# A two-layer encoder trunk on one core: the first norms' sums ahead, x fetched one product later, next weights split in front of the turning

## The chip, the cores and the metric

The kernel runs on one core of one Trainium2 chip. The metric is the device time of one execution in microseconds (us). Five engines work beside each other: PE (TensorE; PEld is its weight load), DVE (VectorE), ACT (ScalarE), POOL (GpSimd), and SP, which here only issues DMAs.

## The reference

A trunk of two layers over x of 512 tokens by 1024 features. Layer 0 is a latent attention (MLA), layer 1 a chunked attention over a shared key/value band; each is followed by a SwiGLU FFN with 2816 hidden features. Every sublayer is x + post_norm(f(pre_norm(x))).

```python
def rms_norm(x, g):
    xf = x.astype(jnp.float32)
    y = xf * lax.rsqrt(jnp.mean(xf * xf, axis=-1, keepdims=True) + EPS)
    return (y * g.astype(jnp.float32)).astype(x.dtype)
...
def swiglu(h, w_gate, w_up, w_down):
    return (jax.nn.silu(h @ w_gate) * (h @ w_up)) @ w_down
...
def mla_mixer(h, cos, sin, w_a, g_q, w_uq, g_kv, w_ukv, w_o):
    a = h @ w_a
    cq, ckv, kr = jnp.split(a, [Q_LORA, Q_LORA + KV_LORA], axis=-1)
    q = (rms_norm(cq, g_q) @ w_uq).reshape(B, S, MLA_HEADS, NOPE_DIM + ROPE_DIM)
...
def shared_kv(x, g_src, w_kv):
    kv = (rms_norm(x, g_src) @ w_kv).reshape(B, S, 2, B_HEADS, B_HEAD_DIM)
```

## The kernel before

**Splits.** Every fp32 operand is split into two fp32r halves: ACT casts the high half (L144, tiles named whi, xh, ph), DVE subtracts it from the source and so makes the low half (L145, names wlo, xl, pl). Where a gain is multiplied in, the lines are L148 on ACT and L149 on DVE. A product is three matmuls on PE (L356 to L358, in the FFN's down stage L1185). So a weight tile must pass a DMA into "raw" or "wd", ACT and DVE before PE can use it.

**Order.** All is written as one program; a framework gives each engine a fixed order of instructions by a running priority number, and puts in the waits. `with first(n)` lowers the number for what is written inside it, so that it goes n places earlier on its engine. Each engine then works its row in order: an instruction that waits holds all that is behind it on that engine.

**The start of layer 0** (L773 to L802). While x and w_a arrive, three banks of a first projection are summed over eight tiles of x. `sx.add(x[k])` squares the tile on ACT (L425, sq) and adds it to acc on DVE (L426). `sx.total()` turns acc on PE with four transposes (L435, tot <- ident, acc), and DVE reduces that (L437) to one sum for each token. `rstd` then makes v (L448) on DVE and v^-0.5 on POOL (L452). The second norm, that of the key/value latent, has its own acc and tot and needs the first result (`rstd_of_scaled`, L458 to L462). The result r is spread over partitions by eight PE transposes (L469, bc <- ident, r), behind the rest of the first projection. In between DVE makes the rotary angles (L804 to L823, rot).

**The down stage of the first FFN** (L1163 to L1187). It is seven products (a Strassen-type scheme) in the order A11, A22, A12, E1, E2, E3, E6, each of 66 matmuls of 128x512 that go in groups (0), (1), (2), (3), (4, 5). Results stand in bank pairs al, ga, be, de. E2, E3 both go to al, E6 goes to be. When a product has ended, `one` copies its two banks into new y tiles (L1246, ACT) or adds them to one (L1252, DVE); E3's first matmul into al needs E2's copy out of al. `during(j, i)` runs behind each group: in E2 it fetches x (eight DMAs of 256 KB on SP's queue, L614), in E6 it puts out the four scalings of the first tokens' y (L1304, ACT; they stand as a list in `later`), and at group 3 `turn(0)`: y's first 256 tokens are turned by 16 PE transposes (L1325, yt), DVE adds gain times yt to x (L1328), and the new x is split (xh, xl). For the other 256 tokens the same follows behind E6, with L1295, L1298 and L1289 for its norm.

**What comes next.** Layer 1 begins with the projection of V from x (w_v, four raw tiles, and the first of in_w_qkb), fed by `feed`, which loads and splits weight tiles in the order of their use; `feed.ahead(n)` splits n tiles ahead. A tile of in_w_qkb is also multiplied by a gain on DVE in place (L306) before its split. Raw tiles share five buffers.

Of the kernel before, what the change touches and what calls it, by code (L numbers as in the profile page):

```python
# [18 lines left out]
D, S, P = 1024, 512, 128  # L19
# [3 lines left out]
QL, KVL = 384, 256  # L23
# [45 lines left out]
def trunk(ctx: ExitStack, tc: tile.TileContext, a, out):  # L69
# [25 lines left out]
    def small(name="sm"):  # L95
        return sp.tile([P, 4], F32, tag="small", name=name_(name))
# [38 lines left out]
    @contextmanager  # L135
    def first(n):

        tc.cur_priority -= n
        yield
        tc.cur_priority += n  # L140
# [46 lines left out]
    class Down:  # L187
# [26 lines left out]
        def fetch(self, to, i, q, tag):  # L214
            n, src = self.width(i), self.src[q, i]
            if tag in ("u", "h"):
                parts = []
                for c in range(0, n, S):
                    t = U(name="wd") if tag == "u" else wide[0].tile([P, S], F32, tag="h", name=name_("wd"), bufs=2 * NF - 4)
                    nc.sync.dma_start(t, src[:, c:c + S])  # L220
                    parts.append(t)
            else:
                t = (wp if tag == "raw" else wide[0]).tile([P, 1024], F32, tag=tag, name=name_("raw"),
                                                           bufs=5 if tag == "raw" else 2)
                nc.sync.dma_start(t[:, :n], src[:, :n])
                parts = [t[:, :n]]
            self.at[to, i] = parts
# [121 lines left out]
    feed = Feed()  # L349
# [29 lines left out]
    def some(gen, n):  # L379
        for _ in range(n):  # L380
            next(gen, None)
# [58 lines left out]
    def rstd(ss, n, eps=EPS):  # L440
        parts = ss if isinstance(ss, list) else [ss]
        m = sum(p.shape[1] for p in parts)
        v = small("v")[:, :m]
        w = m // len(parts)
        for i, p in enumerate(parts):
            o = v[:, i * w:(i + 1) * w]
            if eps is EPS:
                V.tensor_scalar(o, p, 1.0 / n, EPS, op0=OP.mult, op1=OP.add)  # L448
            else:
                V.scalar_tensor_tensor(o, p, 1.0 / n, eps[:, i * w:(i + 1) * w], op0=OP.mult, op1=OP.add)  # L450
        r = small("r")[:, :m]
        nc.gpsimd.tensor_tensor(r, v, mhalf[:, :m], op=OP.pow)  # L452
        return r

    def rstd_of_scaled(ss, n, r0):

        v = small("v2")
        V.tensor_tensor(v, ss, r0, op=OP.mult)  # L458
        V.tensor_tensor(v, v, r0, op=OP.mult)
        r = rstd(v, n)  # L460
        o = small("r2")
        V.tensor_tensor(o, r, r0, op=OP.mult)  # L462
        return o

    def spread(col, first=0):

        b = bank("t", "bc")
        for i in range(col.shape[1]):
            nc.tensor.transpose(b[:, (first + i) * P:(first + i + 1) * P],  # L469
                                col[:, i:i + 1].to_broadcast([P, P]), ident)  # L470
        return b
# [300 lines left out]
    xs, sx = [], Sum()  # L772
# [16 lines left out]
    skv = Sum()  # L789
# [5 lines left out]
        nc.scalar.activation(t, b1[j], AF.Copy, scale=g_kv[:, j:j + 1])  # L795
        ckv.append(t)
    some(rest, 2)
    r0 = rstd(sx.total(), D)
    some(rest, 2)
    rkv = rstd_of_scaled(skv.total(), KVL, r0)  # L800

    quarters = [U(name="rot") for _ in range(2)]  # L802
    pos, ang, da, db, t1, t2 = (quarters[n // 4][:, n % 4 * P:(n % 4 + 1) * P] for n in range(6))
# [37 lines left out]
    rkv = spread(rkv)  # L841
# [380 lines left out]
    class After:  # L1222
# [81 lines left out]
                nc.scalar.activation(t, t, AF.Copy, scale=r)  # L1304

        def during(self, j, i):
            if j == Down.E2 and i == 2:
                self.x = fetch(a["mid"])
                self.split = Split(self.x, None)
            if j == Down.E6 and i == 3:  # L1310
                self.turn(0)
            elif j == Down.E6 and self.later:
                with first(60):
                    self.later.pop(0)()

        def turn(self, h):

# [151 lines left out]
    x, sx = post.x, post.split  # L1469
# [230 lines left out]
```

## Time and profile before

| | |
|---|---|
| median of 3 runs | 1128.0 us (1127.02 to 1128.33) |
| profiled execution, its own time | 1128.58 us |
| its span, first to last instruction | 1126.8 us |
| mean granted TensorE clock | 0.998 |
| PE busy | 1109.3 us, 98% |
| PEld busy | 984.4 us, 87% |
| DVE busy | 932.5 us, 83% |
| ACT busy | 685.3 us, 61% |
| POOL busy | 69.6 us, 6% |

The span lies 1.8 us under the execution's own time; that rest is outside the first and the last instruction. A matmul of 128x512 is shown as 0.39 us long but they follow each other every 0.23 us, so distances between starts tell more than busy time.

### The profile page before, as it was taken

The page shows a single profiled execution, that of the slowest core. Times are in us where ns is not written, and L with a number is a line of the kernel's source. Part 1 is how long each engine was busy: PE and PEld are TensorE (multiplying, and loading weights), DVE is VectorE, ACT ScalarE, POOL GpSimd, SP SyncE. Part 2 cuts the span into 40 slices and gives each one's busy share as a digit, 9 for nine tenths or more (in the row PEclk, how much of TensorE's full clock was granted, in tenths as well). Part 3 has the DMA queues.
Part 4 walks back from the last instruction along what each step waited for, and adds up shares of the span by engine and source line. Part 5 has one row for each costly group of instructions (what it writes and reads, how often), then busy time and mean ns, then how long its engine had stood idle before and what let it go on. Part 6 is the DMA issues. An engine that isn't in the chain of part 4 may idle for free.

```text
span 1126.8 us, 18993 instructions
## 1 busy us (share of the span) xinstructions
PE 1109.3 (98%) x6973; PEld 984.4 (87%) x6973; DVE 932.5 (83%) x1671; ACT 685.3 (61%) x1339; POOL 69.6 (6%) x106
## 2 busy tenths in 40 slices
PE   9999999999999999999999999999999999999997
PEld 6788889999999998887888887779999999998885
DVE  7788737999899889978857977647999899889977
ACT  6476637755555566668536777546755555566675
POOL 2200000000000002400000000000000000002402
PEclk9999999999999999999999999999999999999999
DMA  7332125323332449861456656625323322459923
GB/s 235 110 110 81 70 76 205 132 89 99 105 103 95 140 150 256 138 205 41 165 150 172 154 153 159 170 86 184 134 92 95 113 94 95 141 168 286 171 58 76
DMA packets 62990, 150.85 MB, mean 134 GB/s; under 512 B 8432, under 2 KB 10224, under 8 KB 62896
## 3 DMA queue, kind: packets, MB, share of 16 engines
q1 hardware_dynamic: 55552, 136.61, 38.6%
q0 software_dynamic: 6912, 12.59, 6.8%
q8 instruction: 55, 0.90, 0.3%
q10 hardware_dynamic: 432, 0.44, 0.1%
q14 instruction: 39, 0.32, 0.1%
HBM read 119.52 MB, written 9.63 MB: 115 GB/s over the span
## 4 chain that ended last, share of the span: by engine, by line
PE 44%; DVE 5%; ACT 2%; issue 2%; DMA 1%; POOL 0%; POOLq 0%; DVEq 0%; ACTq 0%
PE al L1434 6%; PE b L356 6%; PE b L357 6%; PE b L358 6%; PE al L1185 4%; PE be L1434 4%; PE be L1185 3%; PE ga L1434 2%; PE pt L508 2%; PE de L1185 1%; PE ga L1185 1%; DVE wlo L145 1%; DVE raw L174 1%; DMA raw<-in_w_pair 1%; PE b L1558 1%
## 5 line engine op out<-in xcount | busy, mean ns | idle before, releaser
L144 ACT CAST whi<-raw 128x1024 fp32r<-128x1024 f32 (+3 forms) x224 | 225.5, 1008 | 227.3 <-PE al L1434 74.5
L145 DVE TENSOR_TENSOR wlo<-raw,whi 128x1024 fp32r<-128x1024 f32 (+3 forms) x224 | 260.7, 1165 | 63.0 <-ACT whi L144 61.2
L1434 PE MATMUL al<-th,whi 128*128 128x256 f32 x432 | 123.4, 286 | 0.2 <-DVE ut L1446 0.2
L1434 PE MATMUL al<-th,wlo 128*128 128x256 f32 x432 | 121.4, 281 | 0.0
L1434 PE MATMUL al<-tl,whi 128*128 128x256 f32 x432 | 121.1, 280 | 0.0
L356 PE MATMUL b<-xh,whi 128*128 128x512 f32 (+1 forms) x304 | 116.8, 384 | 0.2 <-ACT xh L148 0.2
L357 PE MATMUL b<-xl,whi 128*128 128x512 f32 (+1 forms) x304 | 113.3, 373 | 0.4 <-DVE xl L149 0.3
L358 PE MATMUL b<-xh,wlo 128*128 128x512 f32 (+1 forms) x304 | 112.8, 371 | 0.0
L174 DVE TENSOR_TENSOR raw<-raw,raw 128x1024 f32<-128x1024 f32 x72 | 86.5, 1218 | 1.3 <-DMA raw<-in_w_pair 1.1
L1434 PEld LDWEIGHTS al<-th,whi 128*128 128x128 f32 x432 | 81.4, 188 | 3.1 <-DVE ut L1446 1.2
L1434 PEld LDWEIGHTS al<-th,wlo 128*128 128x128 f32 x432 | 81.4, 188 | 0.3 <-DVE wlo L145 0.3
L1434 PEld LDWEIGHTS al<-tl,whi 128*128 128x128 f32 x432 | 81.4, 188 | 0.0
L496 ACT ACTIVATE p<-p,mn 128x128 f32<-128x128 f32 (+1 forms) x96 | 54.0, 562 | 31.8 <-DVE mn L494 31.6
L145 DVE TENSOR_TENSOR ptl<-pt,pth 128x128 fp32r<-128x128 f32 (+1 forms) x96 | 46.2, 485 | 28.8 <-ACT pth L144 23.2
L144 ACT CAST whi<-wd 128x512 fp32r<-128x512 f32 x86 | 49.9, 619 | 26.8 <-PE al L1185 11.9
L145 DVE TENSOR_TENSOR wlo<-wd,whi 128x512 fp32r<-128x512 f32 x86 | 56.3, 685 | 11.5 <-ACT whi L144 11.2
L358 PEld LDWEIGHTS b<-xh,wlo 128*128 128x128 f32 x304 | 57.4, 189 | 8.8
L357 PEld LDWEIGHTS b<-xl,whi 128*128 128x128 f32 x304 | 57.5, 189 | 8.5 <-DVE xl L149 1.9
L356 PEld LDWEIGHTS b<-xh,whi 128*128 128x128 f32 x304 | 57.6, 189 | 8.3 <-ACT xh L148 1.3
L144 ACT CAST pth<-pt 128x128 fp32r<-128x128 f32 (+1 forms) x96 | 40.3, 424 | 28.5 <-PE pt L508 27.8
L1185 PE MATMUL al<-whi,ph 128*128 128x512 f32 x132 | 51.9, 393 | 0.5 <-ACT y L1246 0.5
L1185 PE MATMUL al<-whi,pl 128*128 128x512 f32 x132 | 51.5, 390 | 0.0
(309 smaller groups left out, 3264.3 us busy)
## 6 DMA issues: line engine op xcount, KB each, us to landing
raw<-in_w_pair SPq DMA_DIRECT2D x72, 512.0 KB, 3.8
wd<-in_w_down SPq DMA_DIRECT2D x54, 256.0 KB, 5.8
raw<-in_w_o SPq DMA_DIRECT2D x16, 512.0 KB, 3.6
raw<-in_w_gu SPq DMA_DIRECT2D x16, 512.0 KB, 3.6
raw<-in_w_down SPq DMA_DIRECT2D x16, 512.0 KB, 4.3
raw<-in_w_qkb SPq DMA_DIRECT2D x16, 512.0 KB, 3.6
wd<-in_w_down POOLq DMA_DIRECT2D x22, 256.0 KB, 5.8
wd<-raw POOLq DMA_DIRECT2D x22, 256.0 KB, 4.3
```

What stands on the lines that cost most here:

```text
L144: return (nc.scalar.copy(dst_hi, src), V.tensor_tensor(dst_lo, src, dst_hi.bitcast(F32), op=OP.subtract))
L145: V.tensor_tensor(dst_lo, src, dst_hi.bitcast(F32), op=OP.subtract))
L174: V.tensor_tensor(t, x, y, op=OP.add)
L356: nc.tensor.matmul(o, l[0], r[0], start=start, stop=False)
L357: nc.tensor.matmul(o, l[0], r[1], start=False, stop=False)
L358: nc.tensor.matmul(o, l[1], r[0], start=False, stop=stop)
L496: nc.scalar.activation(p[:, :n], p[:, :n], AF.Exp, bias=mn[:, :1], scale=-1.0, accum_out=self.sums[:, qt:qt + 1])
L508: nc.tensor.transpose(t[:, kt * P:(kt + 1) * P], p[:, kt * P:(kt + 1) * P], ident)
L1185: nc.tensor.matmul(to[e], l[c], r[d], start=j < 4 and k == 0 and n == 0, stop=k == NF // 2 - 1 and n == 2, skip_group_check=True)
L1434: nc.tensor.matmul(o, l[c], r[d], start=first_ and n == 0, stop=k == K2 - 1 and n == 2, skip_group_check=True)
L1558: nc.tensor.matmul(o[:, q_], vv, pth[:, kt, q_], start=kt == 0, stop=False)
```

## The change

Four edits. In the start of layer 0, both norms' chains (from the turning of acc to the power) are written in `first(100)`. In the first down stage the eight loads of x are put out in E3 behind group 1, not in E2 behind group 2. At E6's group 3 the next layer's first weights are split (`feed.ahead(2)`) ahead of `turn(0)`. And the scalings of y lose their `first(60)`. The last layer's stage (AfterLast) has its own `during` and is untouched.

```diff
     some(rest, 2)
-    r0 = rstd(sx.total(), D)
+    with first(100):
+        r0 = rstd(sx.total(), D)
     some(rest, 2)
-    rkv = rstd_of_scaled(skv.total(), KVL, r0)
+    with first(100):
+        rkv = rstd_of_scaled(skv.total(), KVL, r0)
...
         def during(self, j, i):
-            if j == Down.E2 and i == 2:
+            if j == Down.E3 and i == 1:
                 self.x = fetch(a["mid"])
                 self.split = Split(self.x, None)
             if j == Down.E6 and i == 3:
+                feed.ahead(2)
                 self.turn(0)
             elif j == Down.E6 and self.later:
-                with first(60):
-                    self.later.pop(0)()
+                self.later.pop(0)()
```

PE, the start of layer 0: where the first norm's four transposes stood and stand (b is the first projection's bank, tot the turned sum of squares; rows with + are the changed kernel's).

```order
 L358 MATMUL b_12_122<-xh_56_279,wlo_54_273 128x512
 L356 MATMUL b_13_123<-xh_56_279,whi_53_272 128x512
+L435 MATMUL tot_78_347<-ident_87,acc_23_152 128x128 x4
 L357 MATMUL b_13_123<-xl_57_280,whi_53_272 128x512
 L358 MATMUL b_13_123<-xh_56_279,wlo_54_273 128x512
```

The four transposes went 20 rows up, into the middle of a sum over x; the second norm's (acc_71) went up by eight. The place of bc on PE is the same in both.

ACT, the end of E2 and the start of E3, before (whi <- wd are high halves of w_down, ph <- hs those of the hidden tiles, y <- al E2's two copies out of the banks that E3 fills next):

```order
L144 CAST whi_1109_5795<-raw_926_4942 128x512
L144 CAST whi_1113_5815<-wd_973_5188 128x512
L144 CAST whi_1113_5815<-wd_974_5190 128x512
L144 CAST ph_1107_5791<-hs_626_2736 128x512
L144 CAST ph_1111_5811<-hs_674_3097 128x512
L144 CAST whi_1121_5851<-wd_981_5216 128x512
L1246 COPY y_1115_5830<-al_946_5100 128x512
L1246 COPY y_1116_5841<-al_947_5101 128x512
```

The same place in the changed kernel, where every line number behind L800 is greater by two:

```order
L144 CAST whi_1101_5779<-raw_926_4942 128x512
L144 CAST ph_1103_5795<-hs_674_3097 128x512
L144 CAST whi_1105_5799<-wd_973_5188 128x512
L144 CAST whi_1105_5799<-wd_974_5190 128x512
L1248 COPY y_1107_5814<-al_946_5100 128x512
L144 CAST whi_1113_5835<-wd_981_5216 128x512
L144 CAST whi_1113_5835<-wd_982_5218 128x512
L1248 COPY y_1108_5825<-al_947_5101 128x512
```

The first copy now stands ahead of the cast of wd_981, the second behind wd_982. On DVE the in-place product of in_w_qkb (L306, raw_1199) went up by 12 rows to the place right ahead of wlo <- wd_973, the first low half that E3 uses, and on SP the load of that tile went ahead of the eight loads of x.

DVE, the last splits of E6 and the first tokens' turning, before (x <- yt are the additions to x, y <- be E3's late addition, wlo_1188 and wlo_1198 the first and second tile of w_v, wv_1200 the third):

```order
L145 TENSOR_TENSOR wlo_1165_6078<-wd_1016_5334,whi_1164_6077 128x512
L1328 SCALAR_TENSOR_TENSOR x_1099_5775<-yt_1166_6093,gains_70,x_1099_5775 128x256
...
L1328 SCALAR_TENSOR_TENSOR x_1106_5789<-yt_1181_6138,gains_70,x_1106_5789 128x256
L1252 TENSOR_TENSOR y_1116_5841<-y_1116_5841,be_951_5105 128x512
L145 TENSOR_TENSOR xl_1178_6130<-x_1103_5783,xh_1177_6129 128x256
L149 SCALAR_TENSOR_TENSOR wlo_1188_6156<-raw_1160_6053,gains_70,whi_1187_6155 128x512 x2
L145 TENSOR_TENSOR xl_1180_6135<-x_1104_5785,xh_1179_6134 128x256
L149 SCALAR_TENSOR_TENSOR wlo_1198_6208<-raw_1163_6075,gains_70,whi_1197_6207 128x512
```

The same place in the changed kernel, where w_v's first tile is called wlo_1168:

```order
L145 TENSOR_TENSOR wlo_1165_6078<-wd_1016_5334,whi_1164_6077 128x512
L149 SCALAR_TENSOR_TENSOR wv_1200_6227<-raw_1166_6093,gains_70,wv_1200_6227 128x512
L149 SCALAR_TENSOR_TENSOR wlo_1168_6096<-raw_1160_6053,gains_70,whi_1167_6095 128x512 x2
L1330 SCALAR_TENSOR_TENSOR x_1121_5881<-yt_1169_6101,gains_70,x_1121_5881 128x256
...
L1330 SCALAR_TENSOR_TENSOR x_1128_5895<-yt_1184_6146,gains_70,x_1128_5895 128x256
L145 TENSOR_TENSOR xl_1183_6143<-x_1126_5891,xh_1182_6142 128x256
L149 SCALAR_TENSOR_TENSOR wlo_1198_6208<-raw_1163_6075,gains_70,whi_1197_6207 128x512
L145 TENSOR_TENSOR xl_1186_6153<-x_1127_5893,xh_1185_6152 128x256
L149 SCALAR_TENSOR_TENSOR wlo_1198_6208<-raw_1163_6075,gains_70,whi_1197_6207 128x512
```

Three scaled subtractions went ahead of all eight additions to x; the second tile's stand behind them still, as before. On ACT the four pairs of whi casts of E6's last groups and the scalings of y (L1304) are mixed now, where two scalings stood ahead of three ph casts and two ahead of all five whi casts; and on PE 12 more of E6's matmuls stand ahead of the first yt.

## Rows read from the trace of the kernel before

**Rows 1.** The page's busy time by engine, and the granted clock in 40 slices.
```profile
PE 1109.3 (98%) x6973; PEld 984.4 (87%) x6973; DVE 932.5 (83%) x1671; ACT 685.3 (61%) x1339; POOL 69.6 (6%) x106
PEclk9999999999999999999999999999999999999999
```

**Rows 2.** Waits of PEld, whole span: what for, us in total, times, longest.
```profile
PEld b L357 <- DVE wlo L149: 1.7, 1, 1.7
PEld yt L1325 <- ACT y L1289: 1.1, 2, 0.8
PEld bc L469 <- issue: 1.1, 1, 1.1
PEld al L1185 <- ACT y L1246: 0.9, 1, 0.9
PEld be L1185 <- ACT whi L144: 0.7, 1, 0.7
```

**Rows 3.** Timeline of PEld, layer 0's start: start, duration, instruction, [wait <- releaser].
```profile
20.31 0.19 PEld L357 LDWEIGHTS b<-xl,whi 128*128 128x128 f32 x1
...
24.85 0.59 PEld L435 LDWEIGHTS tot<-ident,acc 128*128 128x128 f32 x4
...
26.69 0.59 PEld L435 LDWEIGHTS tot<-ident,acc 128*128 128x128 f32 x4
```

**Rows 4.** Timeline of DVE, the same stretch.
```profile
21.21 0.69 DVE L426 TENSOR_TENSOR acc<-acc,sq 128x512 f32<-128x512 f32 x1
...
27.05 0.68 DVE L437 TENSOR_REDUCE ss<-tot 128x4 f32<-128x512 f32 x1
```

**Rows 5.** Timeline of PE at bc.
```profile
31.25 0.39 PE L358 MATMUL b<-xh,wlo 128*128 128x512 f32 x1
32.30 1.06 PE L469 MATMUL bc<-ident,r 128*128 128x128 f32 x8 [0.66 <-DVE r L462]
```

**Rows 6.** Timeline of POOL, the first power.
```profile
28.09 2.07 POOL L452 TENSOR_TENSOR r<-v,mhalf 128x4 f32<-128x4 f32 x1 [12.53 <-DVE v L448]
```

**Rows 7.** Timeline of PEld, the end of E2; ten rows, then two, left out.
```profile
490.96 0.19 PEld L1185 LDWEIGHTS al<-whi,ph 128*128 128x128 f32 x1
...
493.45 0.19 PEld L1185 LDWEIGHTS al<-whi,pl 128*128 128x128 f32 x1
...
494.92 0.19 PEld L1185 LDWEIGHTS al<-whi,pl 128*128 128x128 f32 x1
```

**Rows 8.** Timeline of ACT, the same stretch.
```profile
490.02 1.14 ACT L144 CAST whi<-wd 128x512 fp32r<-128x512 f32 x2 [2.10 <-PE al L1185]
...
493.42 0.62 ACT L144 CAST whi<-wd 128x512 fp32r<-128x512 f32 x1 [1.22 <-PE al L1185]
493.95 1.07 ACT L1246 COPY y<-al 128x512 f32<-128x512 f32 x2
```

**Rows 9.** Timeline of DVE, E2 and E3.
```profile
485.67 1.22 DVE L145 TENSOR_TENSOR wlo<-raw,whi 128x1024 fp32r<-128x1024 f32 x1
...
500.72 1.22 DVE L306 TENSOR_TENSOR raw<-raw,gains 128x1024 f32<-128x1024 f32 x1
```

**Rows 10.** DMAs issued in 484 to 492 us: count, KB each, median us to landing.
```profile
raw<-in_w_v SPq DMA_DIRECT2D x1, 512.0 KB, 5.2
raw<-in_w_qkb SPq DMA_DIRECT2D x1, 512.0 KB, 6.1
```

**Rows 11.** Timeline of DVE, E6 and after.
```profile
521.98 1.26 DVE L1328 SCALAR_TENSOR_TENSOR x<-yt,gains,x 128x256 f32<-128x256 f32 x3
...
528.45 1.41 DVE L149 SCALAR_TENSOR_TENSOR wlo<-raw,gains,whi 128x512 fp32r<-128x512 f32 x2
...
533.47 0.15 DVE L1295 SCALAR_TENSOR_TENSOR ssv<-ss,ssv 128x2 f32<-128x2 f32 x1
```

**Rows 12.** Timeline of PEld, the first matmuls with w_v.
```profile
527.09 0.41 PEld L356 LDWEIGHTS b<-whi,xh 128*128 128x128 f32 x2
529.25 0.19 PEld L357 LDWEIGHTS b<-wlo,xh 128*128 128x128 f32 x1 [1.75 <-DVE wlo L149]
```

## Prediction

> **What bounds the kernel now.** I read the page's busy times first, then the list of PE's waits, then the timelines around the places that the edits touch. PE is busy 98% of the span, and the granted clock is 9 in every slice [rows 1]. So a microsecond is won only where PE stands still, or lost where it is made to. A matmul shown as 0.39 us long hides short stops; the starts show them better: eleven steps from 490.96 to 493.45 us give 0.2264 us for one [rows 7]. In the list of waits five entries lie where the edits are: 1.7, 1.1, 1.1, 0.9 and 0.7 us, 5.5 us in all [rows 2]. That is nearly all that this change can win, and since PE makes up about 0.1 us of each wait of a weight load (it overlaps the matmul ahead), some 5 us at most.
>
> **Step A, the first norms go first.** Before, PE waits at bc for r: from the last matmul's start at 31.25 to bc's at 32.30 are 1.05 us where 0.23 is the step, so 0.82 us are lost [rows 5]. r is late because the first power starts only at 28.09 and takes 2.07 us [rows 6], behind a tot that PE turns at 24.85 and DVE reduces at 27.05 for 0.68 us [rows 3, 4]. With the sums ahead the power starts some 4 us earlier. The second tot goes up by eight rows: 26.69 - 8 x 0.23 = 24.9 us, plus what PE loses ahead of it (next lines), about 26.5 us. From there 0.6 (tot), 0.7 (reduce), about 0.4 for the small products and at most 2.07 for the second power give r at about 30.3 us, while PE comes to bc at 32.9 us. The wait of 0.82 us goes.
>
> But the first tot now stands 20 rows higher, where PE arrives at 20.31 us [rows 3], and its input, acc with the last square of x, is written by DVE from 21.21 for 0.69 us, until 21.90 [rows 4]. Neither ACT's nor DVE's row ahead of that addition changes. Everything behind tot on PE waits with it: 21.90 - 20.31 = 1.6 us, of which 0.1 is made up; I take 1.5 us. Net of A: 1.5 - 0.82 = **+0.7 us**. Bounds: if later stops swallow the delay, because PE is late where it had to wait for something else anyway, -0.8; if the second tot waits as well, for squares that are themselves late by the 1.6 us, +1.2.
>
> The row shows that PE held its clock through the longest of these stops: the wait of 1.7 us before wlo lies in slices that all show 9 [rows 1, 2]. [...]
>
> **Step B, x fetched later.** Three things move with it. On ACT, E2's first copy out of its banks no longer stands behind a cast of wd that is held until 493.42 by PE's own reading of the old tile [rows 8]. Before, the two copies ran from 493.95 to 495.02 and PE's first matmul of E3 came 494.92 - 493.45 = 1.47 us for three steps of 0.23: 0.79 us lost [rows 7]. In the changed kernel the copy can start when E2's first bank is finished, nine matmuls before the product's end, at about 492.1 (491.4 for that weight load, a step and 0.39 us), while ACT is done with the two casts of 490.02 at 491.2 [rows 8]. The second copy, behind the casts of wd_981 and wd_982 (493.42 to 494.5), ends at about 495.1, when PE, seven steps behind 493.45, wants its bank at 495.0. So the 0.79 us go.
>
> Against it: L306, the in-place product of in_w_qkb, now stands on DVE ahead of E3's first low half. Its tile needs the buffer that DVE's split of 485.67 frees at 486.9 [rows 9]. Landings in that stretch took 5.2 to 6.1 us [rows 10], with the eight loads of x among them, which now come later. A tile landing after L us, 1.2 us of product and 0.6 us of split (half of a split of 128x1024 [rows 9]) give the low half at 488.7 + L, and PE wants it at 493.9: no wait up to 5.2 us, 0.9 us at 6.1. Without x's 2 MB in the queue I take 5.2 or less. Net of B: **-0.8 us**, bounds -0.8 and +0.1.
>
> The loads of x themselves have room: their first use is at 521.98 [rows 11], some 20 us behind the new place.
>
> **Steps C and D, the turning.** Scalings later and next weights earlier work at one place. Before, PE loses 0.7 us for a cast of wd that stands behind the scalings on ACT, 1.7 us for w_v's first low half, and 1.1 us for the second tokens' y [rows 2]; less 0.1 to 0.2 us for each, about 3.1 us. After:
> - The 0.7 us: casts and scalings are mixed, the casts of group 3 first, and 12 more matmuls stand ahead of the first turn. I count the 0.6 us won.
> - The 1.7 us: DVE split w_v's first tile at 528.45, behind eight additions and six low halves of x that began at 521.98 [rows 11], so PE's third matmul with w_v came at 529.25 instead of 527.54 [rows 12]. Now that split comes ahead of them. But the second tile's split stays behind them, and three subtractions of 0.7 us each (half of 528.45's pair) are pushed in front of the additions. These start near 521.98 + 2.1 - 0.6 = 523.5 (0.6 because the casts ahead come earlier), and after 6.5 us of the same work and 0.7 us for the split itself the second tile's low half is there at 530.7. PE, 0.6 us earlier, begins the first tile at 526.5, has four turns (about 0.5 us) and 13 steps (2.9 us) to do, and wants it at 529.9. So of 1.5 us lost some 0.7 remain, and a late addition to x may cost PE 0.2 at its third group of turns.
> - The 1.1 us: y waits for a power, and that for L1295 at 533.47 on DVE [rows 11]. The same splits stand ahead of it, so it can come about 1 us earlier, and PE comes earlier by as much: 1.0 us remain.
>
> Lost after: 0.7 + 0.2 + 1.0 = 1.9 us against 3.1: **-1.2 us**. Bounds: -3.1 when all cover is enough, and +0.2 when the additions, now started later, hold PE's turns as long as w_v did.
>
> **Sum.** +0.7 - 0.8 - 1.2 = -1.3 us. The profiled execution's 1128.58 becomes 1127.3; it stands 0.6 us above the median of 1128.0, so the median becomes **1126.7 us**. Against the noise this is small: 0.2% is 2.26 us, about what a measurement of this kernel can tell from no change.
>
> **Rivals.**
> 1. All covers hold and the new wait at tot is swallowed: -0.8 - 0.8 - 3.1 = -4.7 at the most; half of C's and A's doubt resolved this way gives -3, 1125.0 us. For it: in the attention behind layer 0's start PE has its own waits. Against: DVE is at 83% [rows 1] and busiest in exactly this stretch. Chance 0.2.
> 2. The gains are eaten: A's new wait is 1.5 us, and PE just meets the next late row in the down stage. Then about 0, 1128.0 us, between 1127.3 and 1128.9. For it: three stages in series wait for DVE, and moving one row ahead makes the next late. Chance 0.22.
> 3. Slower: in_w_qkb lands late, and DVE, held by L306, holds all of E3's low halves. The wait is L - 5.2 us; to bring -1.3 + (L - 5.2) above +2.26 us, L must pass 8.8 us, where the longest median of that stretch was 6.1 [rows 10]. At 9.5 us: 1128.0 - 1.3 + 4.3 = 1131.0 us. Chance 0.04.
> 4. [...] Chance 0.02. [...]
>
> **How the numbers follow.** The likeliest, 0.52, is -1.3 us, with its own range from 1126.0 to 1127.4. Faster by over 0.2% are rival 1 and a small tail of the likeliest: 0.22. Slower by over 0.2%: rivals 3 and 4, 0.06. Within: 0.72. The range from 1124.6 to 1128.8 us holds the likeliest, rival 2 and the nearer part of rival 1, and leaves out some 0.15.
>
> **What would show it.** A: no wait at bc, a wait of about 1.6 us at the first tot for L426, and r well ahead of PE. B: al's first matmul in E3 at the normal step, L306 done before 493.3. C: no wait of be for whi, a wait of 0.5 to 1 us for the low half of w_v's second tile, about 1 us for the second y. I am wrong if tot's wait is not there (an earlier square), if L306 holds DVE, or if the turning's waits vanish or come back whole.

## The result: 0.24% slower, and where the time went

The changed kernel takes 1130.35 us (median of 20 runs, 1127.34 to 1133.55) against 1127.49 us of before (20 runs, 1126.06 to 1129.05): the ratio is 1.0024, 95% interval 1.0017 to 1.0031. The forecast was 1126.7 us in a range that ended at 1128.8. The profiled execution took 1133.18 us (span 1131.4), so it shows the loss near its largest: 4.6 us of span.

The page of the changed kernel: busy times, and the granted clock.

```profile
PE 1109.9 (98%) x6973; PEld 985.5 (87%) x6973; DVE 932.8 (82%) x1671; ACT 686.2 (61%) x1339; POOL 71.8 (6%) x106
PEclk9999999999999999999899999999999999999999
```

PE is busy only 0.6 us longer than before [rows 1], so the loss is to be looked for in its waits and its clock. One slice of the clock, from 537 to 566 us, shows 8. The list of PEld's waits (what for, us in total, times, longest) says where:

```profile
PEld yt L1327 <- ACT y L1291: 3.5, 1, 3.5
...
PEld tot L435 <- issue: 2.5, 3, 1.9
...
PEld b L357 <- DVE wlo L149: 1.0, 1, 1.0
...
PEld al L1187 <- DVE wlo L145: 0.8, 1, 0.8
```

Against [rows 2]: w_v's wait fell from 1.7 to 1.0, the waits at bc, at E3's first matmul for y, and at E6 for a cast are gone. New are the waits at tot in layer 0's start, 0.8 us at E3's second matmul, and above all 3.5 us for the second tokens' y, where 1.1 us stood in two waits. A wait at a tot of the second layer, at about 775 us, is 1.7 us here and 0.8 us in before; it goes from 0.8 to 2.1 us in the profiles below, 1.4 in that of the fastest version, so it is not counted for or against the edits.

**Start.** PEld in layer 0's start, then DVE's addition that ends acc:

```profile
20.02 0.19 PEld L356 LDWEIGHTS b<-xh,whi 128*128 128x128 f32 x1
22.10 0.42 PEld L435 LDWEIGHTS tot<-ident,acc 128*128 128x128 f32 x4 [1.89 <-issue]
...
26.91 0.42 PEld L435 LDWEIGHTS tot<-ident,acc 128*128 128x128 f32 x4 [0.48 <-issue]
...
33.12 1.01 PEld L469 LDWEIGHTS bc<-ident,r 128*128 128x128 f32 x8
```

```profile
21.30 0.68 DVE L426 TENSOR_TENSOR acc<-acc,sq 128x512 f32<-128x512 f32 x1
```

acc is ready at 21.98, PE came at 20.25 and waited; the second tot waited too. The wait at bc is gone. In before bc's weight load stood here:

```profile
32.27 0.85 PEld L469 LDWEIGHTS bc<-ident,r 128*128 128x128 f32 x8 [1.05 <-issue]
```

It stands at 33.12 now, 0.85 us later, against the 0.7 forecast.

**E2 to E3.** PEld, then DVE, then the load of in_w_qkb (us to landing):

```profile
494.10 0.19 PEld L1187 LDWEIGHTS al<-whi,ph 128*128 128x128 f32 x1
495.09 0.19 PEld L1187 LDWEIGHTS al<-wlo,ph 128*128 128x128 f32 x1 [0.80 <-DVE wlo L145]
```

```profile
493.21 1.23 DVE L306 TENSOR_TENSOR raw<-raw,gains 128x1024 f32<-128x1024 f32 x1 [3.54 <-DMA raw<-in_w_qkb]
```

```profile
raw<-in_w_qkb SPq DMA_DIRECT2D x1, 512.0 KB, 5.7
```

The copy of y no longer holds PE [rows 7, 8], but L306 waited for in_w_qkb, which was issued at 487.35 and landed 5.7 us later. So the gain was given back in this execution.

**E6 and behind.** This is where the time is. DVE, POOL, ACT and PEld around the second tokens' norm:

```profile
533.25 0.16 DVE L1297 SCALAR_TENSOR_TENSOR ssv<-ss,ssv 128x2 f32<-128x2 f32 x1
533.32 0.75 DVE L149 SCALAR_TENSOR_TENSOR wv<-raw,gains,wv 128x512 fp32r<-128x512 f32 x1
533.98 1.22 DVE L145 TENSOR_TENSOR wlo<-raw,whi 128x1024 fp32r<-128x1024 f32 x1
535.12 0.42 DVE L426 TENSOR_TENSOR acc<-acc,sq 128x256 f32<-128x256 f32 x1
535.45 1.22 DVE L306 TENSOR_TENSOR raw<-raw,gains 128x1024 f32<-128x1024 f32 x1
540.26 1.27 DVE L1330 SCALAR_TENSOR_TENSOR x<-yt,gains,x 128x256 f32<-128x256 f32 x3 [3.58 <-PE yt L1327]
```

```profile
533.55 3.68 POOL L1300 TENSOR_TENSOR r<-ssv,mhalf 128x2 f32<-128x2 f32 x1 [19.50 <-DVE ssv L1297]
```

```profile
537.26 2.56 ACT L1291 ACTIVATE y<-y,r 128x512 f32<-128x512 f32 x4 [4.98 <-POOL r L1300]
```

```profile
534.30 0.19 PEld L356 LDWEIGHTS b<-wv,xh 128*128 128x128 f32 x1
538.03 0.29 PEld L1327 LDWEIGHTS yt<-ident,y 128*128 128x128 f32 x2 [3.54 <-ACT y L1291]
```

In the trace of before DVE and POOL did this at the same place:

```profile
533.54 1.41 DVE L149 SCALAR_TENSOR_TENSOR wv<-raw,gains,wv 128x512 fp32r<-128x512 f32 x2
534.86 1.22 DVE L145 TENSOR_TENSOR wlo<-raw,whi 128x1024 fp32r<-128x1024 f32 x1
536.85 1.27 DVE L1328 SCALAR_TENSOR_TENSOR x<-yt,gains,x 128x256 f32<-128x256 f32 x3 [0.77 <-PE yt L1325]
```

```profile
533.77 1.07 POOL L1298 TENSOR_TENSOR r<-ssv,mhalf 128x2 f32<-128x2 f32 x1 [20.12 <-DVE ssv L1295]
```

L1297 is on time, a little before [rows 11]. But POOL's power of 128x2 elements, 1.07 us in before, takes 3.68 us and ends 0.56 us behind the end of L306. y is scaled from then on, and PE stands. And then the clock falls. Windows of 5 us (busy time and count of PE, PEld, DVE, ACT, POOL, then granted clock, DMA share, GB/s):

```profile
534.00:539.00 5.00, 1.89 (x8) 1.27 (x8) 2.67 (x4) 1.74 (x3) 3.23 (x1) 0.81 0.88 306
539.00:544.00 5.00, 5.00 (x16) 3.99 (x15) 2.72 (x7) 4.59 (x14) 0.00 (x0) 0.51 0.53 198
```

Windows of 1 us show 1.00 at 536 us, 0.54 at 537, 0.50 in each of the five from 538 to 543, 0.55 at 543, and 1.00 again at 544. Means of 0.81 and of 0.51 over 5 us each are then (0.19 + 0.49) x 5 / 0.5 = 6.8 us at 0.50, which costs at most 3.4 us of work; PE still stood idle in the first microsecond of it. At 0.50 PE's matmuls of 128x512 start 0.43 us apart (541.08, 541.51, 541.94 us), where 0.23 is the step.

So the theory, called P: the power waits for the row of two-input operations on DVE, which the two edits of E6 have changed: one operation of L149's kind in place of two, and L426 and L306 in front of the pause. Its rivals: the earlier splits make the norm late (Q); tot's wait is the loss and the rest is noise (R); the power is long because of the loads that land then (S).

### The profile page after: what moved, and what is told of

Read it like the earlier page. It is cut to its first block, busy times and chain, and to the rows that moved or that the text cites. A ratio compares the mean times of both kernels' runs of the same rounds, so it can differ in the third digit from the quotient of the medians.

```text
span 1131.4 us, 18991 instructions
## 1 busy us (share of the span) xinstructions
PE 1109.9 (98%) x6973; PEld 985.5 (87%) x6973; DVE 932.8 (82%) x1671; ACT 686.2 (61%) x1339; POOL 71.8 (6%) x106
## 4 chain that ended last, share of the span: by engine, by line
PE 82%; DVE 7%; ACT 4%; DMA 3%; issue 2%; POOL 1%; POOLq 0%; DVEq 0%; SPq 0%; ACTq 0%
PE al L1436 15%; PE b L356 10%; PE b L357 10%; PE b L358 10%; PE be L1436 8%; PE al L1187 6%; PE ga L1436 4%; PE be L1187 4%; PE de L1187 3%; PE ga L1187 3%; PE pt L508 2%; DVE wlo L145 2%; ACT whi L144 1%; DMA raw<-in_w_akv 1%; DVE raw L174 1%
## 5 line engine op out<-in xcount | busy, mean ns | idle before, releaser
L145 DVE TENSOR_TENSOR wlo<-raw,whi 128x1024 fp32r<-128x1024 f32 (+3 forms) x224 | 261.2, 1167 | 62.5 <-ACT whi L144 60.6
L145 DVE TENSOR_TENSOR ptl<-pt,pth 128x128 fp32r<-128x128 f32 (+1 forms) x96 | 46.2, 486 | 28.7 <-ACT pth L144 23.0
L145 DVE TENSOR_TENSOR wlo<-wd,whi 128x512 fp32r<-128x512 f32 x86 | 56.5, 688 | 10.8 <-ACT whi L144 10.6
L1187 PE MATMUL al<-wlo,ph 128*128 128x512 f32 x132 | 51.5, 390 | 0.4 <-DVE wlo L145 0.4
```

Of the source, the lines that this page charges most:

```text
L145: V.tensor_tensor(dst_lo, src, dst_hi.bitcast(F32), op=OP.subtract))
L1187: nc.tensor.matmul(to[e], l[c], r[d], start=j < 4 and k == 0 and n == 0, stop=k == NF // 2 - 1 and n == 2, skip_group_check=True)
```

## Experiments

All stand against before on the same chip; microseconds won or lost against before are worked out from the ratio. The edits are called a (norms first), b (x fetched later), c (weights split ahead), d (scalings without head start).

**c alone.**

```diff
             if j == Down.E6 and i == 3:
+                feed.ahead(2)
                 self.turn(0)
```

> The kernel before with one edit alone: the next layer's first weights split ahead of the first tokens' turning. Theory P (POOL's second power of this stage, 3.68 us in the changed kernel against 1.07, waits while DVE runs two-input operations back to back): here DVE's row behind the second norm's sum is as before, a scaled subtraction and one split and then a pause, so the power takes 1.0 to 1.7 us and PE's wait for the scaled y stays under 1.5 us; PE's wait for w_v's low half falls from 1.7 to about 1 us; time 0 to 1 us below before. Rival Q (the earlier weight splits themselves push the norm of the second tokens back): the power's input comes 1 to 2 us later, the wait for y grows to 2 to 3 us, time 1 to 2 us above before.

1126.58 us, ratio 0.9993 (0.9984 to 1.0001). The power takes 1.07 us, and PE's wait for w_v's low half falls to 1.0 us. DVE, then POOL:

```profile
533.03 1.41 DVE L149 SCALAR_TENSOR_TENSOR wv<-raw,gains,wv 128x512 fp32r<-128x512 f32 x2
534.35 1.21 DVE L145 TENSOR_TENSOR wlo<-raw,whi 128x1024 fp32r<-128x1024 f32 x1
```

```profile
533.25 1.07 POOL L1298 TENSOR_TENSOR r<-ssv,mhalf 128x2 f32<-128x2 f32 x1 [20.36 <-DVE ssv L1295]
```

Two operations of L149's kind stand behind the sum here, as in before; in the changed kernel only one does. Q falls: the splits stand earlier, and the norm is not late.

**d alone.**

```diff
-                with first(60):
-                    self.later.pop(0)()
+                self.later.pop(0)()
```

> The kernel before with one edit alone: the scalings of y without their head start. DVE's row behind the second norm's sum gets one addition of squares in front of the additions to x, but not the product of in_w_qkb. Theory P: the power may wait for the split and that addition, 1 to 2.3 us; E6's wait for a cast of w_down (0.7 us) goes; time -0.7 to +0.8 us against before. Rival Q (late scalings make the first turning late): a wait of 1 us or more of PE at the first turns, time 1 us above before.

1127.23 us, ratio 0.9999 (0.9990 to 1.0008). E6's wait of 0.7 us for a cast is gone, but w_v's wait grows from 1.7 to 2.1 us, as PE comes earlier to the same late split. The power takes 1.07 us, again beside two operations of L149's kind.

**c and d together.** Both edits above.

> The two edits of E6 together (weights split ahead of the turning, scalings without head start), without the norms' edit and without the later fetch of x. Only with both does the second product of in_w_qkb (128x1024, two inputs) stand on DVE between the second norm's sum and the additions to x. Theory P: the power takes 2 to 3.7 us in most runs, PE's wait for y 2 to 3.5 us, the granted clock falls behind it, time 1 to 3 us above before, with a wide spread, though each edit alone costs nothing. Rival R (the new wait at the first tot makes the loss, the rest is noise): time 1 us below before.

1129.6 us, ratio 1.0019 (1.0005 to 1.0033), from 1125.47 to 1132.47 us. DVE's last operation ahead of the pause, and POOL:

```profile
534.76 1.22 DVE L306 TENSOR_TENSOR raw<-raw,gains 128x1024 f32<-128x1024 f32 x1
```

```profile
532.85 3.68 POOL L1298 TENSOR_TENSOR r<-ssv,mhalf 128x2 f32<-128x2 f32 x1 [19.62 <-DVE ssv L1295]
```

3.68 us again, with the wait for y at 3.5 us and no wait at tot in layer 0's start. Neither edit costs anything alone; together they lose 2 us. R falls. The clock fell here too, less long:

```profile
539.00:544.00 5.00, 5.00 (x20) 3.97 (x19) 3.70 (x11) 4.46 (x16) 0.00 (x0) 0.72 0.58 211
```

**The changed kernel with DVE at rest.** A tiny product on DVE needs the power's result, so DVE must wait for POOL. Nothing reads what it writes.

```diff
             nc.gpsimd.tensor_tensor(r, self.v[:, q], mhalf[:, :n], op=OP.pow)
+            if i >= 2 and self.layer == 0:
+                V.tensor_tensor(self.v[:, q], self.v[:, q], r, op=OP.mult)
             return r
```

> The changed kernel with one tiny DVE operation more, a product of 128x2 with the power's result written right behind the second norm's sum; nothing reads what it writes. DVE so rests, one scaled subtraction behind the sum, until POOL is through. Theory P: the power takes 0.7 to 1.1 us instead of 3.68, PE's wait for y falls from 3.5 to about 0.5 to 0.9 us, the clock stays at 1.00 behind it, and the time falls by 2.5 to 4 us against the changed kernel, to 0.5 us around before. Rival S (the power is long for another reason, such as the loads of w_v that land in these microseconds): the power stays above 2.5 us, the time stays 2 to 3 us above before.

1125.75 us, ratio 0.9988 (0.9979 to 0.9997). DVE waits 0.59 us for r, and the power is back at 1.07 us:

```profile
531.56 0.74 DVE L149 SCALAR_TENSOR_TENSOR wv<-raw,gains,wv 128x512 fp32r<-128x512 f32 x1
532.89 0.16 DVE L1300 TENSOR_TENSOR ssv<-ssv,r 128x2 f32<-128x2 f32 x1 [0.59 <-POOL r L1298]
532.97 1.22 DVE L145 TENSOR_TENSOR wlo<-raw,whi 128x1024 fp32r<-128x1024 f32 x1
```

```profile
531.78 1.07 POOL L1298 TENSOR_TENSOR r<-ssv,mhalf 128x2 f32<-128x2 f32 x1 [19.49 <-DVE ssv L1295]
```

PE's wait for y is 0.9 us, and the clock is 1.00 behind it. An operation that makes DVE do nothing for 0.6 us turns +0.24% into -0.12%, and S falls: the four loads of w_v are issued at the same place (from 529.96 us here, from 531.74 in the changed kernel, 1.8 us ahead of the power in both).

**Which operations hold POOL.** One more operation of 128x512 on DVE, behind the single L149, in two kinds; q is read by nothing.

```diff
+            if i >= 2 and self.layer == 0:
+                q_ = U(name="q")
+                V.scalar_tensor_tensor(q_, self.x[0], self.v[:, i:i + 1], self.x[1], op0=OP.mult, op1=OP.add)
...
+                V.tensor_tensor(q_, self.x[0], self.v[:, i:i + 1].to_broadcast([P, S]), op=OP.add)
```

The first form of the operation:

> The changed kernel with one more DVE operation of 128x512 between the scaled subtraction (L149) behind the second norm's sum and the split of in_w_qkb (L145); the product L306 is then no longer ahead of the additions to x. Here the extra operation is of L149's kind (scalar_tensor_tensor, two inputs in SBUF); its result is read by nothing. Theory P1 (POOL's power is held by tensor_tensor operations with two inputs in SBUF, not by L149's kind): the power takes about 1.07 us, as in the run of the early weight splits alone, because nothing but L149's kind runs in its first 1.2 us. Theory P2 (any back-to-back row of two-input operations holds it, until DVE pauses): DVE pauses only behind the split, 2.5 us behind the sum, so the power takes 2.5 to 3 us.

And the second:

> The same place in the changed kernel, and the same order around it, but the extra operation of 128x512 is a tensor_tensor with two inputs in SBUF; its result is read by nothing. Theory P1: it starts some 0.5 us behind the power, and the split (tensor_tensor too) follows, so POOL is held until the split's end, 2.5 us behind the sum: the power takes 2.5 to 3 us. Theory P2: the same 2.5 to 3 us as with the other kind. Theory P3 (neither: the power was long because of L306 alone): 1.1 us in both.

Each was executed once. DVE and POOL with the scalar_tensor_tensor:

```profile
532.53 0.74 DVE L149 SCALAR_TENSOR_TENSOR wv<-raw,gains,wv 128x512 fp32r<-128x512 f32 x1
533.19 0.74 DVE L1301 SCALAR_TENSOR_TENSOR q<-x,ssv,x 128x512 f32<-128x512 f32 x1
533.85 1.22 DVE L145 TENSOR_TENSOR wlo<-raw,whi 128x1024 fp32r<-128x1024 f32 x1
```

```profile
532.76 1.07 POOL L1298 TENSOR_TENSOR r<-ssv,mhalf 128x2 f32<-128x2 f32 x1 [19.50 <-DVE ssv L1295]
```

With the tensor_tensor:

```profile
530.97 0.74 DVE L149 SCALAR_TENSOR_TENSOR wv<-raw,gains,wv 128x512 fp32r<-128x512 f32 x1
531.64 0.68 DVE L1301 TENSOR_TENSOR q<-x,ssv 128x512 f32<-128x512 f32 x1
532.24 1.22 DVE L145 TENSOR_TENSOR wlo<-raw,whi 128x1024 fp32r<-128x1024 f32 x1
```

```profile
531.20 2.81 POOL L1298 TENSOR_TENSOR r<-ssv,mhalf 128x2 f32<-128x2 f32 x1 [19.49 <-DVE ssv L1295]
```

1126.18 and 1126.69 us. The same place, nearly the same length (0.74 and 0.68 us), and the power takes 1.07 or 2.81 us by the kind of the operation; PE waits 1.2 or 2.9 us for y. (The second input of the tensor_tensor is one column, spread; that this makes the difference is not excluded.) P2 (any row of two-input operations holds POOL until DVE pauses) falls, and so does P3 (L306 alone): here L306 stands behind the pause. P1 (tensor_tensor operations hold POOL) forecast both numbers; the last section says what it leaves out.

**a alone.**

```diff
-    r0 = rstd(sx.total(), D)
+    with first(100): r0 = rstd(sx.total(), D)
     some(rest, 2)
-    rkv = rstd_of_scaled(skv.total(), KVL, r0)
+    with first(100): rkv = rstd_of_scaled(skv.total(), KVL, r0)
```

> The kernel before with the norms' edit alone (both chains with first(100)). By the prediction's step A: PE waits 1.5 to 1.7 us at the first tot, nothing at bc, net +0.7 us; the second tot may wait 0.3 to 0.5 us more, as in the changed kernel's profile: +0.7 to +1.1 us against before. Rival (the delay is swallowed by later stops, or the earlier chain gains more than bc's wait): 0 or below.

1128.8 us, ratio 1.0011 (1.0002 to 1.0020): +1.2 us (0.2 to 2.3). PEld:

```profile
21.77 0.42 PEld L435 LDWEIGHTS tot<-ident,acc 128*128 128x128 f32 x4 [1.58 <-issue]
...
26.77 0.42 PEld L435 LDWEIGHTS tot<-ident,acc 128*128 128x128 f32 x4 [0.65 <-issue]
...
32.95 1.02 PEld L469 LDWEIGHTS bc<-ident,r 128*128 128x128 f32 x8
```

Two waits, 2.2 us, for the one of 1.05 at bc. The rival falls.

**b alone.**

```diff
-            if j == Down.E2 and i == 2:
+            if j == Down.E3 and i == 1:
                 self.x = fetch(a["mid"])
```

> The kernel before with the later fetch of x alone. By the changed kernel's profile the wait of PE for E2's copy (0.9 us) goes, and a wait of up to 0.8 us for the first low half of E3 comes, because in_w_qkb landed 5.9 us behind its issue and L306 stands ahead on DVE: net -0.8 to 0 us against before, by how soon that tile lands in each execution. Rival (the eight loads of x so late disturb loads or writes of the next stage): +1 us or more.

1126.9 us, ratio 0.9991 (0.9982 to 0.9999): -1.0 us (-2.0 to -0.1). The list has no wait of al here: in_w_qkb landed 4.3 us behind its issue, and L306 began at 491.62 us. The changed kernel's 5.7 us was the worse case of the same race: in the eight profiles of kernels with b the tile landed 3.8 to 5.7 us behind its issue.

**The changed kernel again.**

> The changed kernel a second time, for its profile. Theory P: the order on DVE is fixed, so the power is held again until behind L306, 3.5 to 3.8 us, and PE waits 3.3 to 3.6 us for y. Whether the granted clock falls behind that wait, and for how long, may differ, and with it the time by up to 3.4 us; that would be the spread of its runs (1127.3 to 1133.6 us) beside that of before (1126.1 to 1129.1 us). Rival: the hold is a chance of the execution, and the power takes 1 to 2 us this time.

1129.22 us. The power takes 3.68 us once more and PE's wait is 3.5 us, but the clock stays:

```profile
534.00:539.00 5.00, 1.89 (x13) 1.54 (x13) 2.36 (x5) 2.51 (x5) 2.46 (x1) 1.00 0.80 294
539.00:544.00 5.00, 5.00 (x28) 4.08 (x27) 4.32 (x13) 5.00 (x18) 0.00 (x0) 1.00 0.65 239
```

From the power's start (532.78) to the end of the span (1127.5) are 594.7 us, against 597.9 us in the first profile (533.55 to 1131.4), 3.1 us more. Most of that has come by the next tot on PE, here and in the first profile:

```profile
553.90 0.59 PEld L435 LDWEIGHTS tot<-ident,acc 128*128 128x128 f32 x4
```

```profile
557.36 0.59 PEld L435 LDWEIGHTS tot<-ident,acc 128*128 128x128 f32 x4
```

They are 21.1 and 23.8 us behind the power's start, so the fall of the clock cost some 2.7 us; the other 0.4 us are the wait at about 775 us, 1.3 here and 1.7 there. The hold came in all three profiles with this order on DVE, 3.68 us each; the fall behind it comes in some executions and not in others, and why is open. The 20 runs agree: the five with a mean clock of 0.998 or 0.999, which before has too, took 1127.3 to 1129.4 us, the seven with 0.995 or 0.996 1130.1 to 1133.6 us, and the eight with 0.997 1129.0 to 1131.2 us. The mean of the five is 1.0 us above that of before: with the 1.4 us that the edits win without the hold, 2.4 us for the hold alone.

**Versions without a, and DVE's rest alone.** DVE's rest with b, c and d:

> The changed kernel without the norms' edit, and with the small DVE product that makes DVE rest until POOL's power is through. If the norms' edit costs what its run alone showed (+1.2 us), this is 1.0 to 1.3 us under the kernel with the norms' edit and the rest (1125.75): about 1124.6 us, 2.5 us below before. Rival (the norms' delay is swallowed where DVE no longer holds POOL): no difference, 1125.7 us.

1125.42 us, ratio 0.9985 (0.9977 to 0.9994); the 1.2 us that a cost alone are not seen beside the 0.9988 with a, and the forecast of 1124.6 us was missed; why is open. The same with a smaller head start of the first norm only, its edit:

```diff
-    r0 = rstd(sx.total(), D)
+    with first(10):
+        r0 = rstd(sx.total(), D)
```

> As the kernel without the norms' edit and with the rest, but the first norm's sum goes ahead by first(10) alone, and the second norm stays in its old place. The four transposes of acc then stand six rows higher than before, where PE comes at about 23.5 us, behind acc's end at 21.9: no wait at tot, and r some 1 us earlier, so that of the 0.82 us at bc most goes: 1124.0 us. Rival (the first power starts no sooner because DVE's row has the reduction behind the second norm's addition): bc's wait stays, 1124.6 us.

1124.46 us, ratio 0.9977 (0.9967 to 0.9987), the fastest version: 2.6 us below before. But not for the reason expected. The first tot waits no more and the first power is 2 us earlier than before, yet bc waits as long as ever:

```profile
31.79 0.85 PEld L469 LDWEIGHTS bc<-ident,r 128*128 128x128 f32 x8 [1.00 <-issue]
```

The second norm's reduction stands behind the rotary steps on DVE, at 28.83 us. Between these two and the version with all of a (1125.75) the intervals overlap; only that each beats before, and the changed kernel, is shown. Last, DVE's rest in the kernel before:

> The kernel before with the small DVE product alone: DVE rests behind the second norm's sum until POOL is through. In the kernel before the power is not held (1.07 us, two operations of L149's kind run beside it), so theory P expects nothing to win: -0.3 to +0.7 us, the rest of 0.5 us on DVE at most costing a little. Rival (the rest itself is what helps, by giving DVE's row another order): -1 us or more.

1127.06 us, ratio 0.9996 (0.9988 to 1.0005): nothing, as theory P says, since the power is held there no longer than with DVE's rest: 1.07 us in both.

## Why the prediction was wrong

**The step that failed** is the last line of steps C and D: "y waits for a power, and that for L1295 ... 1.0 us remain". L1295 (L1297 now) came at 533.25 us, 0.2 us before its old time, or 0.5 us when counted from the start of E6, where I had put about 1 us, a small miss; but the power was taken at its 1.07 us. With both edits of E6 only one operation of L149's kind is left behind the sum; a row of three tensor_tensor operations follows, two of them (L426 and L306) moved there, and the power takes 3.68 us. The prediction weighs L306 in E3 alone; that its next product moves behind the second tokens' sum stands nowhere in it. The trace of before showed little of a hold at this place, 1.07 us where the same power of 128x2 took 0.69 to 0.83 us elsewhere; but the first power in [rows 6], 2.07 us for 4 columns where the next one took 1.05, was a row that asked for a reason.

With that hold removed, the four edits give -0.12% (-0.21 to -0.03), 1.4 us; the sum was -1.3 us. So the rest of the sum stands, as a sum; that it fits to 0.1 us is luck, since the interval goes from 0.3 to 2.4 us and single terms were off:

- **A**: forecast +0.7, the run alone +1.2. The mechanism was right; the second tot's wait, which I kept as a bound, came true (0.3 to 0.65 us).
- **B**: forecast -0.8, the run alone -1.0. In the changed kernel's profile it was next to nothing, through rival 3's mechanism at 5.7 us of landing, far from the 8.8 us at which it decides; I had taken 5.2 us or less.
- **C and D**: w_v's wait fell from 1.7 to 1.0 us, as said; the cast's wait went, as said; the 0.2 us at the third group of turns came as 0.19 us, and once more at the fourth. Without the hold 0.9 us remain for the second y, where 1.0 was said.
- **Rival 4**, the 0.02 for a lower clock behind tot's wait: that was the author's estimate, and no run shows such a fall. The changed kernel waits 1.89 us at the first tot, and every window of 2 us from 20 to 28 us shows 1.00. The clock did fall, but behind the wait of 3.5 us for y, and 6.8 us at 0.50 cost 2.7 us. The sum went by the row in which the clock held through 1.7 us; a 9 for a slice of 28 us could hide some 5 us at 0.50, but windows of 2 us around that wait show 1.00. Of the three profiles of the wait of 3.5 us two show a lower clock in the window behind it (0.51 and 0.72), the third does not (1.00).
- **Rivals 1 and 2** did not come: the waits neither vanished nor just evened out.

So +0.24% is: the four edits' -0.12% and 0.36%, some 4 us, for the hold: 2.6 us of the power's own (3.68 less 1.07), and the rest by the fallen clock in a part of the executions.

## What to carry to other kernels

A tiny operation on the way of a whole stage is priced by what runs beside it, not by its own row (the second tokens' power took 1.07, 2.81 or 3.68 us here): when an edit moves work on DVE, look which operations now stand behind the sum that POOL needs, and of what kind. Two edits that are each free can lose together: each alone left two operations of L149's kind behind the sum, between which POOL got in, and both together left one. Run the pair, not only the parts. And a stop of PE that grows beyond the longest in the profile of before has no price there: the clock may go with it, as here behind 3.5 us in two profiles of three, where the longest wait of before was 1.7.

## What the runs showed of the hardware

In four of these profiles, where the rows show it, the second tokens' power ends 0.55 to 0.56 us behind the end of a DVE operation: of L306 (536.67 and 537.23 us in the changed kernel), of the split L145 with the extra tensor_tensor (533.46 and 534.01), of the first L149 with the extra scalar_tensor_tensor (533.27 and 533.83), and of the only L149 where DVE then rests (532.30 and 532.85). So in these runs L149's kind held POOL as well, until its end; but POOL got in between two of that kind (1.07 us), and not ahead of a tensor_tensor that followed at once (2.81 and 3.68 us). Whether the power or the split began first did not decide it there: the power of the changed kernel had started at 533.55, ahead of the split at 533.98, and still ended 0.56 us behind the second of the two operations that follow the split, 3.68 us for 1.07. In the two forms above the power went with the kind of the operation, 1.07 and 2.81 us.

What decides at such a boundary stays open. In the start of layer 0 of the changed kernel a power ends 0.9 us behind the split at 26.20 us although the addition L426, a tensor_tensor, had begun at 26.11. With DVE's rest, where nothing follows that split at once, it is 0.88 us (24.70 and 25.58): there L426 did not lengthen the power.
